# Three plain query groups in place of four, and another order of the closing steps, in a decoder step of two layers

## The chip, the cores and the metric

The kernel runs on one core of a Trainium2 chip. The metric is the device time of one execution in microseconds (us), as the median of several runs; less is better. All arithmetic is in fp32: each matrix operand is split into a high and a low part, and a product is made of three matmuls, high by high, high by low, low by high.

The core's engines run side by side and wait for each other by semaphores: TensorE (PE in the profile, its weight loads PEld), VectorE (DVE), ScalarE (ACT), GpSimd (POOL) and SyncE (SP, which here issues DMAs).

## What is computed

One step of a decoder with mixers of two kinds, over 1024 prompt rows and 8 decoded rows, 2048 wide. Layer 0 (kind A) is a pooling mixer, and layer 1 (kind B) is attention in a window of 128 with its own queries and gates and with keys and values that are projected once. Each ends in a layer norm.

```python
def pool_layer(x, prefix, pos, w_in, w_grp, scale, w_out, g_ln, b_ln):
    z = x @ w_in
    u, gate = z[..., :D_POOL], z[..., D_POOL:]
    d, new_state = multiscale_pool(u, prefix, pos)
    d = jnp.einsum('btgc,gce->btge', d.reshape(B, T, N_POOL_GROUPS, POOL_GROUP), w_grp)
    d = d.reshape(B, T, D_POOL) * scale
    y = (d * jax.nn.silu(gate)) @ w_out
    return layer_norm(ALPHA * x + y, g_ln, b_ln), new_state

def attn_layer(x, pos, kb, vb, k_pos, q_pos, blocked, w_in, sinks, w_out, g_ln, b_ln):
    z = x @ w_in
    q = rope_partial(z[..., :D_ATTN].reshape(B, T, N_HEADS, HEAD_DIM), pos)
    gate = z[..., D_ATTN:]
    ...
    o = attn_core(q, kb, vb, q_pos, k_pos, sinks).reshape(B, T, D_ATTN)
    y = (o * jax.nn.silu(gate)) @ w_out
    return layer_norm(ALPHA * x + y, g_ln, b_ln)
```

The reference calls these once each for the prompt and for the decoded rows, with `shared_kv` (a projection to 4 heads of 64) between them. Outputs are the two results, the new pool states, and the last 128 keys and values.

## The kernel before

The rows are taken in two chunks: chunk 0 has 512 columns in a matmul (rows of the prompt stand along the columns), chunk 1 has 520, the 8 decoded rows among them. The program is one list of stages, `PHASES` (L50): `ai` (input product and pooling), `ao` (output product and layer norm), `bi` (queries, gates and attention), `bo` (output product and layer norm), each with its chunk, and for `ai` and `bi` the range of groups. A group of `bi` is two query tiles and their two gate tiles, of 128 rows each; a tile holds two heads.

A product of a weight with a chunk has two forms. `PLAIN` (L57) names the stages that use the first.

- Plain: `unit` (L672) takes a tile of 128 output rows in 48 matmuls of 512 columns (L686 to L688, the three of one split pair); a group is four units, 192 matmuls.
- Seven products: `seven` (L582) makes, from a block of 2 by 2, seven products in place of eight (the scheme of Strassen). Each product has 24 matmuls (L658 to L660) on half the columns, 256 in chunk 0 and 260 in chunk 1. The seven weights are sums of the four blocks of the weight; they are made by additions (`first_pair`, L346, for chunk 0, which stores them for chunk 1 too) and split into high (L488 on ACT) and low (L503 on DVE). The products are put together by copies on ACT and additions on DVE (`p0` to `p6`, L597 to L631). A group is two such pairs, 336 matmuls. Groups that are plain for chunk 0 have the sums for chunk 1 made in `plain_pair` (L293).

Instructions go to each engine in program order; what sets the order is the code that writes them out. Work beside the products (layer norm of the other chunk, transposes, sums of weights) is in generators. `end` (L527) is called at the end of each product, and four times in a plain unit, and takes one step of the generator at the head whenever `self.i / self.every` passes a whole number, `self.every` being products per step. It is set in `run` (L2148): 3 at the start of each stage, and other values in some.

```python
if self.side and int(self.i / self.every) != int((self.i - 1) / self.every) and room >= self.room:
```

`ln_gen` (L912) is the layer norm of a chunk: its variance's reciprocal root is `rstd` (L901: a lookup on ACT, L904, and three steps on DVE, L905 to L907), then eight pieces of 128x1024 are subtracted and multiplied (L999, L1000 on DVE), scaled (L991 on ACT) and stored. In stage `bo` of chunk 1 it runs for chunk 0, and stores `y0`. There, `shifted` (L1267) sums a pair's columns (`mean` L1276, `less` L1280, `square` L1286, `add` L1291, L1292).

The end of the program is `phase_end` (L1308), for the last three output pairs of chunk 1. Its products follow the table `TAIL`, and `steps` ties closing steps to single products. The columns of chunk 1 are in two halves: A (the last 260, done last) and Bh. For the first, `affine` (L1368: `affine1` subtracts and multiplies on DVE, L1374 and L1375; `affine2` scales and adds on ACT, L1382, and stores, L1383) writes the normed result in the transposed layout. For the last, the results are transposed back: `scale` (L1394, ACT) multiplies by the norm's weights, `turn` (L1477, PE) transposes, `sums_a` (L1432, PE) forms the sums over all rows of the values and of their squares, `moments` (L1437) makes from them the mean and the reciprocal root (L1448 to L1457, L1445), `last_rows` (L1485, PE) subtracts the mean, and `evict` (L1491) multiplies into the output rows, on DVE (L1497) or ACT (L1502), and stores (L1498). `spare` and `last_four` (L1504) do the decoded rows.

## Time and profile before

| | us |
|---|---|
| median of three runs | 2330.92 (2330.76 to 2331.43) |
| the profiled execution | 2332.49 |
| its span, first to last instruction | 2330.7 |

The profile is of one execution. A share is of its span. In a row of the timeline stand the start in us, the duration, the engine, the line, the operation, what it wrote from what (128x260 is partitions by elements) and how often; brackets at its end tell how long the engine stood idle before it and who ended that. `pD`, `pO` and `pS` are accumulators of PE, `m` is a buffer in the on-chip memory. Rows that follow from a view by stretch have the busy time of each engine in that stretch. The granted clock is that of TensorE as a share of full speed. The table below gives the page's costliest lines on DVE and ACT, which stand beside the products.

| line, engine | what | count | busy us |
|---|---|---|---|
| L503, DVE | low part of a weight | 674 | 814.6 |
| L488, ACT | high part of a weight | 674 | 701.5 |
| L778, DVE | low part of an activation | 120 | 147.1 |
| L769, ACT | high part of an activation | 120 | 125.8 |
| L346, DVE | sum of weights | 88 | 107.6 |

### The profile page before, as it was taken

What the parts mean: (1) busy time and instruction counts of PE and PEld (TensorE: products, weight loads), DVE (VectorE), ACT (ScalarE), POOL (GpSimd) and SP (SyncE); (2) the same over time, 40 slices, a digit from 0 to 9 for tenths busy, and PEclk for the clock granted to TensorE, in tenths of its full rate; (3) what the DMA queues carried; (4) which work ended last, traced back from release to release, by engine and by line L of the source; (5) the groups of instructions that cost most, each with busy time, mean ns of one, the idle gap of its engine ahead of it and who ended that gap; (6) DMA issues with size and microseconds to landing.
All of it is one profiled execution on the core that took longest, in us unless ns stands there. A gap on an engine that the chain in (4) does not pass through costs nothing. (4 is left out here: it accounts for less than half of the span.)

```text
span 2330.7 us, 49775 instructions
## 1 busy us (share of the span) xinstructions
PE 2293.2 (98%) x19960; PEld 2199.7 (94%) x19960; DVE 1908.7 (82%) x2422; ACT 1350.4 (58%) x2492; POOL 205.7 (9%) x411
## 2 busy tenths in 40 slices
PE   8999999999999999999999999999999999999997
PEld 6899999999999999999788799999999999999997
DVE  8787998777878878988996888897676777889887
ACT  4444445544546546655465566785776678646556
POOL 0111110010000000000111111100000000000001
PEclk9999999999999999999999999999999999999999
DMA  8668789988899989999886666798777778799785
GB/s 293 221 228 312 267 293 356 330 302 297 278 325 320 340 280 325 323 385 345 274 333 240 241 220 236 240 321 288 246 245 221 221 229 307 243 361 379 250 303 198
DMA packets 250919, 665.04 MB, mean 285 GB/s; under 512 B 25760, under 2 KB 106432, under 8 KB 250688
## 3 DMA queue, kind: packets, MB, share of 16 engines
q1 hardware_dynamic: 205216, 496.79, 63.5%
q0 software_dynamic: 45472, 165.07, 18.4%
q8 instruction: 156, 2.56, 0.4%
q14 instruction: 75, 0.61, 0.1%
HBM read 466.66 MB, written 185.59 MB: 280 GB/s over the span
## 5 line engine op out<-in xcount | busy, mean ns | idle before, releaser
L658 PE MATMUL pD<-m,m 128*128 128x260 f32 (+1 forms) x4752 | 1346.2, 283 | 5.5 <-DVE m L619 3.9
L660 PE MATMUL pD<-m,m 128*128 128x260 f32 (+1 forms) x4752 | 1339.1, 282 | 3.3 <-DVE m L503 3.1
L659 PE MATMUL pD<-m,m 128*128 128x260 f32 (+1 forms) x4752 | 1339.3, 282 | 0.0
L658 PEld LDWEIGHTS pD<-m,m 128*128 128x128 f32 x4752 | 895.3, 188 | 10.9 <-issue 3.2
L660 PEld LDWEIGHTS pD<-m,m 128*128 128x128 f32 x4752 | 895.8, 189 | 4.0 <-DVE m L503 3.9
L659 PEld LDWEIGHTS pD<-m,m 128*128 128x128 f32 x4752 | 895.6, 188 | 0.5
L503 DVE TENSOR_TENSOR m<-m,m 128x1024 fp32r<-128x1024 f32 x674 | 814.6, 1220 | 72.7 <-ACT m L488 48.3
L488 ACT CAST m<-m 128x1024 fp32r<-128x1024 f32 x674 | 701.5, 1048 | 253.1 <-DVE m L346 77.7
L686 PE MATMUL pD<-m,m 128*128 128x512 f32 x448 | 179.7, 401 | 8.0 <-ACT m L769 8.0
L687 PE MATMUL pD<-m,m 128*128 128x512 f32 x448 | 177.6, 396 | 0.7 <-DVE m L778 0.7
L688 PE MATMUL pD<-m,m 128*128 128x512 f32 x448 | 177.2, 396 | 0.0
L778 DVE TENSOR_TENSOR m<-m,m 128x1024 fp32r<-128x1024 f32 (+1 forms) x120 | 147.1, 1229 | 9.5 <-ACT m L769 7.9
L631 ACT COPY m<-pD 128x260 f32<-128x260 f32 (+1 forms) x83 | 31.0, 374 | 189.8 <-PE pD L660 189.7
L769 ACT CAST m<-m 128x1024 fp32r<-128x1024 f32 (+1 forms) x120 | 125.8, 1051 | 10.3 <-DVE m L503 4.1
L346 DVE TENSOR_TENSOR m<-m,m 128x1024 f32<-128x1024 f32 x88 | 107.6, 1223 | 6.9 <-DMA m<-in_wia 4.2
L686 PEld LDWEIGHTS pD<-m,m 128*128 128x128 f32 x448 | 85.0, 190 | 27.9 <-ACT m L769 8.0
L687 PEld LDWEIGHTS pD<-m,m 128*128 128x128 f32 x448 | 85.0, 190 | 20.6 <-DVE m L778 1.9
L688 PEld LDWEIGHTS pD<-m,m 128*128 128x128 f32 x448 | 84.8, 189 | 19.8
L619 DVE TENSOR_TENSOR m<-pD,m 128x260 f32<-128x260 f32 (+1 forms) x86 | 36.5, 425 | 80.9 <-PE pD L660 80.8
L1798 ACT ACTIVATE m<-m,sm 128x128 f32<-128x128 f32 x256 | 99.2, 390 | 0.0
L1820 ACT ACTIVATE m<-m,sm 128x128 f32<-128x128 f32 (+1 forms) x320 | 93.9, 372 | 8.9 <-DVE sm L1806 5.5
L1088 PE MATMUL pD<-m,m 128*128 128x260 f32 (+1 forms) x528 | 91.2, 323 | 0.0
(249 smaller groups left out, 2157.2 us busy)
## 6 DMA issues: line engine op xcount, KB each, us to landing
m<-in_wia SPq DMA_DIRECT2D x124, 512.0 KB
m<-in_wib SPq DMA_DIRECT2D x120, 512.0 KB
swia<-m POOLq DMA_DIRECT2D x64, 512.0 KB, 5.0
m<-swia SPq DMA_DIRECT2D x64, 512.0 KB
m<-swoa SPq DMA_DIRECT2D x64, 512.0 KB
swib<-m POOLq DMA_DIRECT2D x64, 512.0 KB, 5.8
m<-swib SPq DMA_DIRECT2D x64, 512.0 KB
m<-swob SPq DMA_DIRECT2D x56, 512.0 KB
```

Source lines behind the costliest of these rows:

```text
L346: self.nc.vector.tensor_add(s[out].a[:, :1024], s[x].a[:, :1024], s[y].a[:, :1024])
L488: self.nc.scalar.copy(hi.r[:, :1024], self.stream[self.cast].src().a[:, :1024])
L503: self.nc.vector.tensor_sub(lo.r[:, :1024], s.src().a[:, :1024], hi.a[:, :1024])
L658: nc.tensor.matmul(ps[:, :TH], wh[:, s], h, start=new and k == 0, stop=False, skip_group_check=on)
L659: nc.tensor.matmul(ps[:, :TH], wh[:, s], l, start=False, stop=False, skip_group_check=on)
L660: nc.tensor.matmul(ps[:, :TH], wl[:, s], h, start=False, stop=k == 7, skip_group_check=on)
L686: nc.tensor.matmul(ps[:], wh[:, s], h, start=par == 0 and k == 0, stop=False)
L687: nc.tensor.matmul(ps[:], wh[:, s], l, start=False, stop=False)
L688: nc.tensor.matmul(ps[:], wl[:, s], h, start=False, stop=par == 1 and k == 7)
L769: self.nc.scalar.copy(h.r[:, :n], s.a[:, :n])
L778: self.nc.vector.tensor_sub(l.r[:, :n], s.a[:, :n], h.a[:, :n])
L1798: nc.scalar.activation(x["s3"][:, i, :], x["s3"][:, i, :], AF.Exp, bias=nm[:, i : i + 1], scale=0.125, accum_out=rs[:, i : i + 1],)
```

## The change

Three parts. First, the plain `bi` stage of chunk 0 has groups 0 to 2 in place of 0 to 3; group 3 joins the seven-product stage, which has five groups in place of four. Second, `every` has two new values: 1.4 in that seven-product stage (3 before), and 2.4 in `bo` of chunk 1 (3 before). Third, the closing steps of `phase_end` are put in another order: the last product is followed at once by its addition, squares, the transposes and the column sums; two of the subtract-and-multiply steps and their scaling go behind the moments; `scale(y)` goes into the moments; of the eight evictions three, not four, are on DVE.

```diff
@@ -48,8 +48,8 @@
-    ("ai", 0, (0, 1)), ("ai", 0, (1, 4)), ("ai", 1, (0, 4)), ("ao", 0, None), ("ao", 1, None), ("bi", 0, (0, 4)),
-    ("bi", 0, (4, 8)), ("bi", 1, (0, 8)), ("bo", 0, None), ("bo", 1, None),
+    ("ai", 0, (0, 1)), ("ai", 0, (1, 4)), ("ai", 1, (0, 4)), ("ao", 0, None), ("ao", 1, None), ("bi", 0, (0, 3)),
+    ("bi", 0, (3, 8)), ("bi", 1, (0, 8)), ("bo", 0, None), ("bo", 1, None),
@@ -1434,7 +1434,7 @@
-        def moments():
+        def moments(between):
...
             nc.scalar.mul(X[hi], mb[hi, A2], -1.0)
+            between()
@@ -1493,13 +1494,14 @@
+            if k % 2 and (b, k) != (0, 3):
+                nc.vector.tensor_scalar(y, X[b, k][:], r, None, op0=ALU.mult)
+            else:
+                nc.scalar.activation(y, X[b, k][:], AF.Copy, scale=r)
             if k % 2:
-                nc.vector.tensor_scalar(y, X[b, k][:], r, None, op0=ALU.mult)
...
-            else:
-                nc.scalar.activation(y, X[b, k][:], AF.Copy, scale=r)
@@ -1543,15 +1545,13 @@
             (y, 5): [
-                lambda: square(x, A), lambda: affine(0, Bh), lambda: affine(x, Bh), lambda: spare(3), lambda: scale(3),
+                lambda: square(x, A), lambda: affine(0, Bh), lambda: spare(3), lambda: scale(3),
             ],
             (y, 6): [
-                lambda: add(x, A), lambda: rest(z, A), lambda: affine(y, Bh), lambda: spare(x), lambda: scale(x),
+                lambda: rest(z, A), lambda: add(x, A), lambda: affine(x, Bh), lambda: spare(x), lambda: scale(x),
             ],
-            (z, 5): [lambda: square(y, A), lambda: affine(z, Bh), lambda: spare(4), lambda: scale(4)],
-            (z, 6): [
-                lambda: square(z, A, 0), lambda: add(y, A), lambda: scale(z, (0,), True),
-            ],
+            (z, 5): [lambda: square(y, A), lambda: affine1(y, Bh), lambda: spare(4), lambda: scale(4)],
+            (z, 6): [lambda: square(z, A, 0), lambda: add(y, A), lambda: affine2(y, Bh)],
@@ -1567,30 +1567,27 @@
         square(z, A, 1)
-        spare(y)
-        spare(z)
-        scale(z, (1,))
-        scale(y)
-        affine1(1, Bh)
-        affine2(1, Bh)
         X[0, 0], X[0, 1] = self.psD(), self.psD()
         turn(0, 0, 8)
         sums_a(())
         sums_a((0,))
         sums_a((1,))
+        spare(y)
+        spare(z)
+        scale(z, (0, 1), True)
+        affine1(z, Bh)
         X[0, 2], X[0, 3] = self.psW(), self.psW()
+        X[1, 0], X[1, 1] = self.psO(), self.psD()
+        moments(lambda: scale(y))
+        affine2(z, Bh)
         turn(0, 8, 16)
-        X[1, 0], X[1, 1] = self.psO(), self.psD()
         turn(1, 0, 8)
-        affine1(2, Bh)
-        moments()
...
-        affine2(2, Bh)
...
-        affine1(3, Bh)
+        affine1(1, Bh)
@@ -1599,10 +1596,15 @@
         last_rows(1, (3,))
+        affine1(2, Bh)
+        affine2(1, Bh)
+        for k in range(3):
+            evict(1, k)
+        affine2(2, Bh)
+        affine1(3, Bh)
+        evict(1, 3)
         affine2(3, Bh)
         affine1(4, Bh)
-        for k in range(4):
-            evict(1, k)
         affine2(4, Bh)
@@ -2207,6 +2209,8 @@
+            elif (kind, c) == ("bi", 0):
+                self.every = 1.4
@@ -2218,7 +2222,7 @@
-                self.every = 3
+                self.every = 2.4
```

The lines of the new kernel stand one or two later than those of before from L1450 on.

PE, at the place where the third plain group ends after the change (`pD` is a unit's or product's accumulator, `m` are weight and activation). Before, the plain units go on:

```order
L686 MATMUL pD_14584<-m_1487_12538,m_1680_14433 128x512
L687 MATMUL pD_14584<-m_1495_12608,m_1680_14433 128x512
L688 MATMUL pD_14584<-m_1487_12538,m_1684_14481 128x512
L686 MATMUL pD_14584<-m_1496_12610,m_1680_14433 128x512
L687 MATMUL pD_14584<-m_1502_12649,m_1680_14433 128x512
L688 MATMUL pD_14584<-m_1496_12610,m_1684_14481 128x512
```

After:

```order
L686 MATMUL pD_14497<-m_1524_12791,m_1684_14348 128x512
L687 MATMUL pD_14497<-m_1528_12824,m_1684_14348 128x512
L688 MATMUL pD_14497<-m_1524_12791,m_1691_14451 128x512
L658 MATMUL pD_14671<-m_1658_14088,m_1692_14453 128x256
L659 MATMUL pD_14671<-m_1664_14187,m_1692_14453 128x256
L660 MATMUL pD_14671<-m_1658_14088,m_1695_14499 128x256
```

Where a unit of 512 columns stood, the first product of a seven-product pair begins, on 256.

DVE, in stage `bo` of chunk 1, where `ln_gen` takes its reciprocal root (`pD` is a product's accumulator, the 128x1040 rows are the column sums of a pair). Before:

```order
L503 TENSOR_TENSOR m_2848_26616<-m_2829_26465,m_2844_26578 128x1024
L1280 TENSOR_TENSOR m_2795_26196<-m_2795_26196,m_2846_26612 128x1040
L503 TENSOR_TENSOR m_2852_26658<-m_2834_26505,m_2849_26618 128x1024
L1280 TENSOR_TENSOR m_2787_26156<-m_2787_26156,m_2846_26612 128x1040
L503 TENSOR_TENSOR m_2857_26693<-m_2838_26539,m_2853_26660 128x1024
L1291 TENSOR_TENSOR m_2767_26029<-m_2787_26156,m_2795_26196 128x1040
L1292 TENSOR_TENSOR m_2850_26644<-m_2850_26644,m_2854_26687 128x1040
L905 TENSOR_TENSOR m_2845_26606<-m_2793_26192 128x512
L906 SCALAR_TENSOR_TENSOR m_2845_26606<-m_2845_26606 128x512
L907 SCALAR_TENSOR_TENSOR m_2793_26192<-m_2845_26606,m_2793_26192 128x512
L619 TENSOR_TENSOR m_2855_26689<-pD_26572,m_2846_26612 128x260
```

After:

```order
L503 TENSOR_TENSOR m_2860_26789<-m_2842_26644,m_2857_26757 128x1024
L1280 TENSOR_TENSOR m_2805_26365<-m_2805_26365,m_2858_26785 128x1040
L905 TENSOR_TENSOR m_2854_26745<-m_2811_26401 128x512
L906 SCALAR_TENSOR_TENSOR m_2854_26745<-m_2854_26745 128x512
L907 SCALAR_TENSOR_TENSOR m_2811_26401<-m_2854_26745,m_2811_26401 128x512
L503 TENSOR_TENSOR m_2864_26835<-m_2846_26678,m_2861_26791 128x1024
L1280 TENSOR_TENSOR m_2799_26329<-m_2799_26329,m_2858_26785 128x1040
L503 TENSOR_TENSOR m_2869_26870<-m_2850_26712,m_2865_26837 128x1024
L1291 TENSOR_TENSOR m_2779_26202<-m_2799_26329,m_2805_26365 128x1040
L1292 TENSOR_TENSOR m_2862_26817<-m_2862_26817,m_2866_26864 128x1040
L619 TENSOR_TENSOR m_2867_26866<-pD_26751,m_2858_26785 128x260
```

L905 to L907 stand behind the first L1280 now, ahead of two splits, the second L1280, L1291 and L1292; L619 stands behind all of them in both.

ACT, at the same place. Before:

```order
L1276 ACTIVATE m_2846_26612<-pO_26645 128x260
L1276 ACTIVATE m_2846_26612<-pD_26649 128x260
L608 COPY m_2846_26612<-pD_26572 128x260
L488 CAST m_2853_26660<-m_2838_26539 128x1024
L1286 ACTIVATE m_2854_26687<-m_2795_26196 128x1040
L614 COPY m_2855_26689<-pD_26545 128x260
L488 CAST m_2858_26695<-m_2842_26574 128x1024
L1286 ACTIVATE m_2850_26644<-m_2787_26156 128x1040
L904 ACT_TABLE_LOAD
L904 ACTIVATE m_2793_26192<-m_2845_26606 128x512
```

After:

```order
L1276 ACTIVATE m_2858_26785<-pO_26818 128x260
L1276 ACTIVATE m_2858_26785<-pD_26822 128x260
L904 ACT_TABLE_LOAD
L904 ACTIVATE m_2811_26401<-m_2854_26745 128x512
L608 COPY m_2858_26785<-pD_26751 128x260
L488 CAST m_2865_26837<-m_2850_26712 128x1024
L1286 ACTIVATE m_2866_26864<-m_2805_26365 128x1040
L614 COPY m_2867_26866<-pD_26718 128x260
L488 CAST m_2870_26872<-m_2855_26753 128x1024
L1286 ACTIVATE m_2862_26817<-m_2799_26329 128x1040
```

The table load and L904 moved from behind the second L1286 to right behind the second L1276.

DVE, behind the last product, from its addition L612 to the moments (L1449). Before:

```order
L612 TENSOR_TENSOR m_2954_27600<-pD_28018,m_2954_27600 128x260
L1346 TENSOR_TENSOR m_2767_26029<-m_2767_26029,m_2936_27431 128x2x260
L1347 TENSOR_TENSOR m_2850_26644<-m_2850_26644,m_2974_27788 128x2x260
L629 TENSOR_TENSOR m_2954_27600<-pD_28056,m_2954_27600 128x260
L1374 TENSOR_TENSOR m_2975_27790<-m_2975_27790,m_2987_27914 128x2x260
L1375 TENSOR_TENSOR m_2975_27790<-m_2975_27790,m_2987_27914 128x2x260
L1374 TENSOR_TENSOR m_2976_27792<-m_2976_27792,m_2987_27914 128x2x260
L1375 TENSOR_TENSOR m_2976_27792<-m_2976_27792,m_2987_27914 128x2x260
L1449 TENSOR_TENSOR m_2995_28142<-m_2846_26612 128x260
L1451 SCALAR_TENSOR_TENSOR m_2995_28142<-pD_28109,m_2995_28142 128x260
```

After:

```order
L612 TENSOR_TENSOR m_2967_27793<-pD_28189,m_2967_27793 128x260
L1346 TENSOR_TENSOR m_2779_26202<-m_2779_26202,m_2949_27624 128x2x260
L1347 TENSOR_TENSOR m_2862_26817<-m_2862_26817,m_2986_27974 128x2x260
L629 TENSOR_TENSOR m_2967_27793<-pD_28221,m_2967_27793 128x260
L1374 TENSOR_TENSOR m_2967_27793<-m_2967_27793,m_2999_28095 128x2x260
L1375 TENSOR_TENSOR m_2967_27793<-m_2967_27793,m_2999_28095 128x2x260
L1449 TENSOR_TENSOR m_3007_28287<-m_2858_26785 128x260
L1452 SCALAR_TENSOR_TENSOR m_3007_28287<-pD_28265,m_3007_28287 128x260
```

One subtract-and-multiply pair (L1374, L1375) stands between the last addition, L629, and the moments, where there were two.

## The prediction

> **What bounds the kernel now.** I read three views: the page's busy times, the list of what TensorE (PE) waited for, and the busy time of each engine by stretch of the span. In the last, each row gives the stretch, then PE, weight load (PEld), VectorE (DVE), ScalarE (ACT) and GpSimd busy with their counts, then the granted clock, the DMA share and GB/s.
>
> ```profile
> PE 2293.2 (98%) x19960; PEld 2199.7 (94%) x19960; DVE 1908.7 (82%) x2422; ACT 1350.4 (58%) x2492; POOL 205.7 (9%) x411
> PE pD L658 <- DVE m L619: 3.9, 4, 1.3
> PE pO L1863 <- ACT m L1833: 1.8, 1, 1.8
> ```
>
> PE is busy for 98% of the span, and what it waited for comes to single microseconds, so the time is in essence the sum of what PE issues, a few named stalls, and the end behind the last product. DVE, at 82%, is second; where a stretch has it near full, it can take over. So I price the change in three places: the group that changes its form, the last output stage (where side work is taken oftener), and the end.
>
> **1. One plain group becomes a seven-product group.** The plain form takes 192 matmuls of 512 columns for a group; the other takes two pairs of seven products of 24 matmuls, 336, of 256 columns. Their paces are seen in stretches that hold only one kind:
>
> ```profile
> 75.00:100.00 25.00, 25.00 (x110) 20.28 (x109) 17.15 (x16) 10.01 (x11) 2.13 (x4) 1.00 0.53 175
> 875.00:900.00 25.00, 25.00 (x214) 25.00 (x214) 17.01 (x17) 12.85 (x17) 0.53 (x1) 1.00 0.86 296
> 1435.00:1460.00 25.00, 25.00 (x286) 24.72 (x285) 22.59 (x30) 18.45 (x48) 3.63 (x8) 1.00 0.66 228
> ```
>
> A count takes in matmuls still running at an edge; two are left off. Then 25/108 = 231.5 ns for 512 columns and 25/212 = 118 ns for 256. 192 x 0.2315 = 44.4 us go, 336 x 0.118 = 39.6 us come: **-4.8 us** on PE. The attention's own matmuls (L1761, L1863) are the same in number. What hides the rest of the group's work is DVE: the seven-product form adds six weight splits (L488 on ACT, L503 on DVE) and its additions. In the third row, inside the seven-product groups of this stage, PE is busy for all 25.00 us with DVE at 22.59, so there is cover of some 10%, also for the two pieces of the layer norm of chunk 1 that now fall behind the first seven-product group. If that cover goes, the group takes what DVE takes; the nearest row is the first below, where DVE had 24.76 of 25 and PE lost 0.47 us. Bounds: -4.8 and, with two such stretches, -3.8. I take -4.8, by the third row, which is the stage that the new group joins.
>
> Shortly before the plain stage ends there is a stall in the attention between its units, and behind it a slow clock:
>
> ```profile
> 1326.65 0.33 PE L1863 MATMUL pO<-m,m 64*64 64x128 f32 x2 [1.82 <-ACT m L1833]
> 1327.38 0.37 PE L1863 MATMUL pO<-m,m 64*64 64x64 f32 x2 [0.28 <-DVE m L1834]
> ...
> 1325.00:1330.00 5.00, 3.07 (x36) 2.43 (x37) 3.37 (x4) 3.15 (x10) 0.64 (x2) 0.74 1.03 371
> 1330.00:1335.00 5.00, 5.00 (x49) 3.90 (x48) 4.90 (x10) 1.79 (x5) 1.45 (x3) 0.92 1.03 396
> 1335.00:1360.00 25.00, 24.53 (x222) 23.64 (x220) 24.76 (x28) 19.92 (x45) 3.15 (x7) 1.00 0.67 244
> ```
>
> The two waits make 2.10 us; the granted clock is 0.74 and 0.92 in the next two stretches, so (0.26 + 0.08) x 5 = 1.7 us of clock were lost. The same instructions stand there in the same order after the change, one group earlier: I price it at nothing. Its ends are -3.8 (stall and clock loss gone) and +2.1 (the stall doubled); the value taken is the one that the same order gives, and either end needs a cause that the rows don't show.
>
> [...]
>
> **2. The last output stage takes layer-norm steps every 2.4 products, not every 3.** The one step with a new wait is the reciprocal root (L904 on ACT, L905 to L907 on DVE). In the trace of before it stands behind the last additions of a pair:
>
> ```profile
> 2188.95 0.39 ACT L1276 ACTIVATE m<-pD 128x260 f32<-128x260 f32 x1
> 2194.12 1.28 ACT L904 ACT_TABLE_LOAD   x1
> 2195.41 0.63 ACT L904 ACTIVATE m<-m 128x512 f32<-128x512 f32 x1
> ...
> 2189.37 1.24 DVE L1280 TENSOR_TENSOR m<-m,m 128x1040 f32<-128x1040 f32 x1 [1.98 <-ACT m L1276]
> 2196.26 0.68 DVE L905 TENSOR_TENSOR m<-m 128x512 f32<-128x512 f32 x1
> 2198.31 0.42 DVE L619 TENSOR_TENSOR m<-pD,m 128x260 f32<-128x260 f32 x1
> 2198.88 0.36 PE L658 MATMUL pD<-m,m 128*128 128x260 f32 x1 [1.34 <-DVE m L619]
> ```
>
> Now the table load and L904 come on ACT right behind the second L1276, and L905 on DVE behind the first L1280 alone. ACT would end L904 at 2189.34 + 1.28 + 0.63 = 2191.25; DVE ends the first L1280 at 2190.61. So L905 waits some 0.65 us, with the splits and additions of the product queued behind it on DVE, and L619, which releases PE, behind those. The work ahead of L619 is otherwise the same sum in another order. So the stall of 1.34 us grows to about 2.0: **+0.7 us**. Ends: -1.3 in place of +0.7, if the order lets the stall go altogether (DVE stood idle 1.98 us ahead of L1280, and a step that comes sooner could lie there), and +1.7 more, if the clock falls as it did at 2.10 us; both are rivals.
>
> [...]
>
> Then the eight steps that follow (L999, L1000: subtract and multiply a 128x1024 piece) come closer together:
>
> ```profile
> 2205.89 1.22 DVE L999 TENSOR_TENSOR m<-m,m 128x1024 f32<-128x1024 f32 x1
> 2208.29 1.22 DVE L503 TENSOR_TENSOR m<-m,m 128x1024 fp32r<-128x1024 f32 x1
> ...
> 2205.00:2230.00 25.00, 25.00 (x212) 25.00 (x211) 24.68 (x23) 17.05 (x24) 1.07 (x2) 1.00 0.87 310
> 2230.00:2255.00 25.00, 25.00 (x211) 25.00 (x210) 22.83 (x22) 14.27 (x22) 1.58 (x2) 1.00 0.95 342
> ```
>
> A piece takes DVE 2.40 us. A product is 24 matmuls at 25/209 = 0.12 us, 2.87 us, so 25 us hold 8.7 products: 2.9 pieces before, 3.6 after, 0.7 x 2.40 = 1.7 us more DVE work on 24.68 and 22.83, in the mean 25.5 of 25. That is 0.5 us over in 25, while the eight pieces last (8 x 2.4 x 2.87 = 55 us): 1.1 us; products that are ahead in their buffers take up a part. Ends: 0 (by the second row, 24.5 of 25) and 3.0 (by the first, 26.4). I take **+0.3**: the rows' mean holds other extra work (L1280 among it) that does not come in every pair.
>
> **3. The end.** Before, PE transposes behind the last product, waits for DVE, and forms the column sums; the sums lead through ACT and DVE to the moments:
>
> ```profile
> 2306.08 0.60 PE L1477 MATMUL pD<-cst,m 128*128 128x128 f32 x4
> 2307.66 0.66 PE L1477 MATMUL pD<-cst,m 128*128 128x128 f32 x4 [0.98 <-DVE m L612]
> 2308.26 2.46 PE L1432 MATMUL pD<-m,jr 128*128 128x260 f32 x10
> 2311.61 1.58 PE L1432 MATMUL pD<-m,jr 128*128 128x260 f32 x6 [0.89 <-ACT m L1343]
> ...
> 2294.29 1.22 DVE L999 TENSOR_TENSOR m<-m,m 128x1024 f32<-128x1024 f32 x1
> 2308.73 0.42 DVE L629 TENSOR_TENSOR m<-pD,m 128x260 f32<-128x260 f32 x1
> 2314.35 0.35 ACT L1448 COPY m<-pD 128x260 f32<-128x260 f32 x1
> 2318.03 0.87 DVE L1445 TENSOR_TENSOR m<-m,m 32x256 fp32r<-32x256 f32 x2
> ```
>
> The last addition (L629) comes 2.65 us behind the first transpose, since DVE is that far behind: the last of the eight pieces (2294.29) and affine pairs (L1374, L1375) stand ahead of it. The closer pace of part 2 takes the piece from there, and the change puts two of the affine steps behind the moments. So neither the 0.98 nor the 0.89 us should be left: eight transposes from 2306.1 to 2307.0, sixteen sums at (2.46 + 1.58)/16 = 0.25 us to 2311.0, L1448 at 2311.1 (3.25 us sooner). From L1448 to the end of L1445 it was 4.55 us, now to 2315.65. What was moved must then be done:
>
> ```profile
> 2318.93 0.70 DVE L1374 TENSOR_TENSOR m<-m,m 128x520 f32<-128x520 f32 x1
> 2320.28 1.40 DVE L1497 TENSOR_SCALAR m<-pD,sm 128x512 f32<-128x512 f32 x2
> 2321.60 0.21 DVE L1508 TENSOR_TENSOR m<-m 128x64 f32<-128x64 f32 x1
> 2322.52 0.69 DVE L1374 TENSOR_TENSOR m<-m,m 128x520 f32<-128x520 f32 x1
> ...
> 2323.98 1.10 ACT L1382 ACTIVATE m<-m,prm 128x260 f32<-128x260 f32 x2 [0.95 <-DVE m L1375]
> 2324.67 0.99 SPq L1498 DMA_DIRECT2D out_y1a<-m  x2
> 2325.75 0.56 SPq L1383 DMA_DIRECT2D out_y<-m  x1
> 2322.00:2323.00 1.00, 0.00 (x0) 0.00 (x0) 0.93 (x4) 1.00 (x2) 0.00 (x0) 1.00 1.00 401
> 2328.00:2329.00 1.00, 0.00 (x0) 0.00 (x0) 0.00 (x0) 0.00 (x0) 0.00 (x0) 0.50 0.86 307
> ```
>
> An affine pair is 1.35 us (from 2318.93 to 2320.28), an eviction 0.66, the four small steps 0.92. Behind the moments DVE now has four pairs, three evictions and the small steps: 5.4 + 2.0 + 0.9 = 8.3 us, to 2323.95; the last two L1382 on ACT 1.10, to 2325.05; the last store is issued some 0.65 us sooner than at 2325.75. Then the queue: before, two stores of 0.5 MB went out at 2324.67 just ahead of it, and transfers ran until about 2328.9 at 400 and 307 GB/s. Now an affine pair and its scaling lie between the last large store and the last one, so up to 0.5 MB/0.4 = 1.3 us of queue goes; I take 0.9. Sum **-1.6**. Ends: -0.6 (issue alone) and -2.0.
>
> **Sum.** -4.8 + 0.7 + 0.3 - 1.6 = -5.4. The profiled execution took 2332.49 us (span 2330.7 and 1.79 around it), 1.57 above the median of 2330.92: 2332.49 - 5.4 = 2327.1, and less the same 1.57, **2325.5**. The 1.57 is about one slow-clock stretch, which may not be in every execution.
>
> **The rivals.**
> - The clock falls at the longer L619 stall, too. For it: it comes to 2.0 us, and 2.10 sufficed. Against it:
>
> ```profile
> 2190.00:2215.00 25.00, 23.66 (x197) 23.48 (x196) 23.78 (x24) 16.68 (x22) 1.07 (x2) 1.00 0.80 262
> ```
>
> with 1.34 us of stall inside, the clock stayed at 1.00. It gives +1.7: 2327.2. Chance 0.21.
> - The swap or the end brings less, DVE being the bound in the new group (-3.8) or behind the moments (-0.6, or evictions on ACT late): +1.0 to +2.0, some 2327.8 with a part of part 2's upper end. Chance 0.15.
> - ACT pauses behind the table load before L904 begins, for about another 1.28 us as the load itself takes; L905, the additions and L619 are later by as much: +1.3, 2326.8. The row of L904 shows no such pause. Chance 0.02. [...]
> - The L619 stall vanishes and the end takes its full -2.0: -0.7 - 1.3 - 0.4 = -2.4, 2323.1. Chance 0.12.
> - Slower: in the last output stage DVE at 26.4 of 25 becomes the bound, and what it is late is not spread but gathers in stalls of 2 us at every second of the eight pieces. Each then costs 2.1 and a slow stretch of 1.7: 4 x 3.8 = 15.2, 2340. It decides from a lateness of some 2 us at one product; the excess by the first row is 3.0 us over all eight, 0.4 each, which speaks against it. Chance 0.04.
> - The change does nothing: the group is no shorter since PE then waits for weights (the DMA share is 0.66 in the stage). 2331. Chance 0.02.
>
> **How the numbers follow.** The forecast's own case has 0.44. What a measurement of this kernel can tell from no change is about 0.2%, 4.7 us: faster means below 2326.3. Of the first case 0.39 lies below that and 0.05 above, by its terms' ends; with the 0.12 that is 0.51 faster; 0.05 + 0.21 + 0.15 + 0.02 + 0.02 = 0.45 the same; 0.04 slower. The range goes from 2322.8, just beyond the third rival, to 2329.2: the second rival with the upper end (3.0) of the piece term half taken. It leaves out the slower case, no effect, and some 0.1 on the edges.
>
> **What would show it.** In the changed kernel's profile: 64 fewer each of L686 to L688, and PE busy for 25.00 of 25 in the seven-product groups of the first attention stage; the stall of about 2 us at L1863 with the slower clock behind it, about a group's time earlier; L905 waiting for L904 and L619 releasing PE after about 2 us, with the clock at 1.00 there; the last L999 before 2270; sums right behind the transposes, L1448 some 3 us closer to the last product, and the last landing 1.6 us closer. The forecast is wrong if PE shows waits for DVE in stretches where it now has none, or if the clock falls a second time in the last stage.

## The result and the profile after

The changed kernel took 2338.27 us (median of 8; 2334.41 to 2341.26) against 2332.32 for the kernel before (median of 8; 2330.76 to 2334.48): ratio 1.0025, 95% interval 1.0016 to 1.0034. A second comparison gave 2336.07 against 2332.52, ratio 1.0020 (1.0011 to 1.0029). It is slower by 3.5 to 6 us, where 5.4 less was forecast. Of the rivals, the first (the clock falls at the longer L619 stall) happened in the profile, but it gave 2327; most of the loss is elsewhere.

The profiled execution took 2339.09 us, its span 2337.3, 6.6 more than that of before. First what TensorE waited for, as groups of line and releaser (total, count, longest), in the changed kernel:

```profile
PE pD L658 <- DVE m L619: 6.1, 5, 2.5
PE pD L660 <- DVE m L503: 4.7, 2, 2.7
PE pO L1865 <- ACT m L1835: 4.1, 2, 2.9
```

The same three groups were 3.9, 3.1 (two waits, the longest 2.6) and 1.8 us before; the third is L1863 there. The page's busy share of PE is 98% in both kernels, and cannot show this: it counts a matmul at half clock as busy (4.46 of the 5.00 us from 1235 us, at a clock of 0.50). So the second view is the stalls one by one, with the granted clock (third number from the end) of the 5 us behind each, in the changed kernel:

```profile
1232.89 0.33 PE L1865 MATMUL pO<-m,m 64*64 64x128 f32 x2 [2.90 <-ACT m L1835]
1235.54 1.88 PE L1763 MATMUL pS<-m,m 64*64 64x192 f32 x20 [0.80 <-DVE m L1731]
1279.49 0.33 PE L1865 MATMUL pO<-m,m 64*64 64x128 f32 x2 [1.25 <-ACT m L1835]
2035.54 0.46 PE L658 MATMUL pD<-m,m 128*128 128x256 f32 x1 [2.45 <-DVE m L619]
2108.23 0.39 PE L660 MATMUL pD<-m,m 128*128 128x256 f32 x1 [2.69 <-DVE m L503]
2205.23 0.36 PE L658 MATMUL pD<-m,m 128*128 128x260 f32 x1 [2.07 <-DVE m L619]
...
1230.00:1235.00 5.00, 1.58 (x32) 1.15 (x32) 2.10 (x4) 4.12 (x8) 0.10 (x1) 0.85 0.16 62
1235.00:1240.00 5.00, 4.46 (x65) 3.75 (x66) 3.61 (x5) 2.63 (x4) 0.00 (x0) 0.50 0.32 105
1280.00:1285.00 5.00, 4.79 (x35) 3.85 (x36) 4.97 (x6) 0.99 (x6) 0.65 (x2) 0.66 1.04 363
2035.00:2040.00 5.00, 4.46 (x25) 4.49 (x26) 4.97 (x7) 0.99 (x1) 1.06 (x2) 0.66 1.01 375
2105.00:2110.00 5.00, 2.31 (x20) 2.10 (x19) 4.96 (x7) 1.27 (x2) 0.58 (x2) 1.00 1.04 392
2205.00:2210.00 5.00, 4.77 (x27) 4.80 (x28) 4.97 (x6) 0.92 (x2) 0.00 (x0) 0.66 0.81 296
```

Four of the six are followed by a slow clock: (0.15 + 0.50) x 5 = 3.2 us behind the first pair, 0.34 x 5 = 1.7 behind each of three others. Two rows of before, at the places where the fourth and fifth stand now, for comparison; both had the clock at 1.00 behind them:

```profile
2034.25 0.36 PE L658 MATMUL pD<-m,m 128*128 128x256 f32 x1 [1.33 <-DVE m L619]
2103.34 0.39 PE L660 MATMUL pD<-m,m 128*128 128x256 f32 x1 [0.56 <-DVE m L503]
```

The end came out nearly as long as forecast (what made it so is another matter, see the parts alone). From the timeline of the changed kernel:

```profile
2313.98 1.04 PE L1478 MATMUL pD<-cst,m 128*128 128x128 f32 x8
2314.85 3.67 PE L1432 MATMUL pD<-m,jr 128*128 128x260 f32 x16
2318.12 0.38 ACT L1448 COPY m<-pD 128x260 f32<-128x260 f32 x1 [2.18 <-PE pD L1432]
2321.82 0.87 DVE L1445 TENSOR_TENSOR m<-m,m 32x256 fp32r<-32x256 f32 x2
2330.24 2.38 SPq L1383 DMA_DIRECT2D out_y<-m  x2
2334.00:2335.00 1.00, 0.00 (x0) 0.00 (x0) 0.00 (x0) 0.00 (x0) 0.00 (x0) 0.50 0.37 98
```

Transposes and sums run through. From the first transpose to the end of the span it is 2337.3 - 2313.98 = 23.3 us, before 2330.7 - 2306.08 = 24.6: -1.3. All that precedes the transposes is therefore 7.9 us later (2313.98 - 2306.08). In that: the swap's matmuls, -4.8; stalls of the first attention stage, 2.90 + 0.80 + 1.25 and two of 0.28 for 2.10, +3.4; the clock there, 4.9 for 1.7, +3.2; the two stalls in the first chunk's output stage +3.3 and the clock +1.7; L619 in the last stage +0.7 and the clock +1.7. That is 9.2; early in the program a slow stretch of before (1.7 us, behind a stall at 355 us, which neither kernel's change touches) is missing in this profile, which leaves 7.5 of 7.9. That is one execution: in a second profile of the same kernel (span 2333.9) the transposes begin 4.7 us later than in the first profile of before.

### The profile page after: what moved, and what is told of

Same layout as the page of the kernel before. It is cut to its first block, busy times and chain, and to the rows that moved or that the text cites. A ratio compares the mean times of both kernels' runs of the same rounds, so it can differ in the third digit from the quotient of the medians.

```text
span 2337.3 us, 50083 instructions
## 1 busy us (share of the span) xinstructions
PE 2293.3 (98%) x20104; PEld 2208.7 (94%) x20104; DVE 1915.0 (82%) x2427; ACT 1358.0 (58%) x2504; POOL 204.3 (9%) x411
## 3 DMA queue, kind: packets, MB, share of 16 engines
q0 software_dynamic: 45472, 165.07, 18.3%
## 5 line engine op out<-in xcount | busy, mean ns | idle before, releaser
L658 PE MATMUL pD<-m,m 128*128 128x260 f32 (+1 forms) x4864 | 1379.2, 284 | 8.7 <-DVE m L619 6.1
L660 PE MATMUL pD<-m,m 128*128 128x260 f32 (+1 forms) x4864 | 1371.4, 282 | 4.9 <-DVE m L503 4.7
L659 PE MATMUL pD<-m,m 128*128 128x260 f32 (+1 forms) x4864 | 1371.5, 282 | 0.0
L658 PEld LDWEIGHTS pD<-m,m 128*128 128x128 f32 x4864 | 917.0, 189 | 14.4 <-issue 6.3
L660 PEld LDWEIGHTS pD<-m,m 128*128 128x128 f32 x4864 | 917.8, 189 | 5.6 <-DVE m L503 5.5
L659 PEld LDWEIGHTS pD<-m,m 128*128 128x128 f32 x4864 | 917.4, 189 | 0.5
L503 DVE TENSOR_TENSOR m<-m,m 128x1024 fp32r<-128x1024 f32 x680 | 820.8, 1218 | 70.2 <-ACT m L488 46.6
L686 PE MATMUL pD<-m,m 128*128 128x512 f32 x384 | 154.7, 403 | 8.0 <-ACT m L769 8.0
L687 PE MATMUL pD<-m,m 128*128 128x512 f32 x384 | 152.9, 398 | 0.5 <-DVE m L778 0.5
L688 PE MATMUL pD<-m,m 128*128 128x512 f32 x384 | 152.7, 398 | 0.0
L769 ACT CAST m<-m 128x1024 fp32r<-128x1024 f32 (+1 forms) x120 | 125.8, 1052 | 10.9 <-DMA m<-in_x 4.0
L346 DVE TENSOR_TENSOR m<-m,m 128x1024 f32<-128x1024 f32 x96 | 117.3, 1222 | 10.2 <-DMA m<-in_wia 6.1
L619 DVE TENSOR_TENSOR m<-pD,m 128x260 f32<-128x260 f32 (+1 forms) x88 | 37.2, 423 | 84.3 <-PE pD L660 84.2
L686 PEld LDWEIGHTS pD<-m,m 128*128 128x128 f32 x384 | 73.3, 191 | 25.3 <-ACT m L769 8.0
L1088 PE MATMUL pD<-m,m 128*128 128x260 f32 (+1 forms) x528 | 91.2, 323 | 0.0
L687 PEld LDWEIGHTS pD<-m,m 128*128 128x128 f32 x384 | 73.4, 191 | 17.4 <-DVE m L778 1.0
L688 PEld LDWEIGHTS pD<-m,m 128*128 128x128 f32 x384 | 73.2, 191 | 17.1
```

The lines of the kernel that those rows point to most:

```text
L346: self.nc.vector.tensor_add(s[out].a[:, :1024], s[x].a[:, :1024], s[y].a[:, :1024])
L503: self.nc.vector.tensor_sub(lo.r[:, :1024], s.src().a[:, :1024], hi.a[:, :1024])
L658: nc.tensor.matmul(ps[:, :TH], wh[:, s], h, start=new and k == 0, stop=False, skip_group_check=on)
L659: nc.tensor.matmul(ps[:, :TH], wh[:, s], l, start=False, stop=False, skip_group_check=on)
L660: nc.tensor.matmul(ps[:, :TH], wl[:, s], h, start=False, stop=k == 7, skip_group_check=on)
L686: nc.tensor.matmul(ps[:], wh[:, s], h, start=par == 0 and k == 0, stop=False)
```

## The experiments

Theory A in them is that the swap pays what was forecast, and that two losses take it away: a weight that comes late at the end of the plain stage, and the pace of 2.4 in the last stage, each dearer by a slow clock behind its stall. A ratio is to the kernel before in the same comparison, with its 95% interval; 11 or 12 executions of each version, 33 to 35 of the kernel before. An interval reaches some 2 us to each side, so a difference of some 2 us between two versions lies at the edge of the noise.

| kernel | median us | before | ratio |
|---|---|---|---|
| swap and 1.4 alone | 2334.68 | 2333.44 | 1.0002 (0.9994 to 1.0010) |
| pace 2.4 alone | 2331.62 | 2333.44 | 0.9992 (0.9983 to 1.0000) |
| closing order alone | 2331.62 | 2333.44 | 0.9990 (0.9981 to 0.9998) |
| the same, again | 2332.09 | 2332.65 | 0.9996 (0.9987 to 1.0004) |
| whole change, again | 2336.07 | 2332.52 | 1.0020 (1.0011 to 1.0029) |
| whole, pace 3 | 2333.70 | 2332.52 | 1.0006 (0.9997 to 1.0015) |
| whole, no swap | 2334.27 | 2332.52 | 1.0006 (0.9997 to 1.0014) |
| whole, loads later | 2333.06 | 2332.52 | 1.0002 (0.9993 to 1.0011) |
| whole, loads later, start one sooner | 2332.29 | 2332.65 | 1.0000 (0.9991 to 1.0008) |
| whole, loads later, pace 3 | 2329.50 | 2332.65 | 0.9986 (0.9977 to 0.9994) |
| swap, loads later | 2328.89 | 2332.65 | 0.9987 (0.9978 to 0.9995) |

### The parts alone

The swap, as a diff against before:

```diff
-("bi", 0, (0, 4)), ("bi", 0, (4, 8))
+("bi", 0, (0, 3)), ("bi", 0, (3, 8))
...
+            elif (kind, c) == ("bi", 0):
+                self.every = 1.4
```

> Of the change, only the third-to-fourth plain group's swap (PHASES) and the value 1.4 in the seven-product stage. Theory A: the swap itself pays its 4.8 us of matmuls, but the end of the plain stage now has a stall of about 3 us of TensorE (a weight that lands late) and two slow stretches of the clock in place of one; in sum +1 us against before (-2 to +3). Rival B: the swap pays its 4.8 us, and the loss of the whole change sits in the last output stage: -4.8 us.

The swap alone is +1.2 us in the median, and its interval takes in no change: A's number, not B's. Its profile has the same stall, with two steps of slow clock behind it. From the waits of TensorE (two waits, the longest 2.5 us):

```profile
PE pO L1863 <- ACT m L1833: 3.8, 2, 2.5
```

The pace alone:

```diff
-                self.every = 3
+                self.every = 2.4
```

> Of the change, only the pace 2.4 in place of 3 in the last output stage. Theory A: the stall at L619 grows from 1.3 to 2 us, with a slow stretch of 1.7 behind it in some executions: +0.5 to +2.5 us. Rival B: the layer-norm pieces make DVE the bound there, +8 us or more. A second rival: the stall goes, -1.3.

The result is 0.9992 (0.9983 to 1.0000), a small gain if any. A and B missed; the second rival's -1.3 lies in the interval, but its mechanism failed: the stall did not go. The profile has 2.27 us at L619 in place of 1.34, with a slow stretch behind it. What it gains is at the end of the program (below).

The closing order alone is the third part of the change's diff.

> Of the change, only the order of the closing steps. Theory A and B alike: from the last product's end to the last instruction 23.3 in place of 24.6 us, as in the profile of the whole change: -1.3 us. Rival: without the closer pace DVE is still behind at the last product, and the transposes and sums wait as before: -0.3 us.

> The closing order alone, for the second time. Theory A: 1.3 to 1.8 us under before. Rival: the first result was chance; within 0.5 us of before.

0.9990 and 0.9996: between -2.3 and -0.9 us, so -1.3 fits, and the rival of -0.3 is not excluded. The profiles say more. From the first transpose behind the last product I took the time to SyncE's last store and to the end of the span (us; one profile each, two where two numbers stand):

| kernel | to the last store | to the end |
|---|---|---|
| before | 19.7, 19.7 | 24.6, 24.9 |
| closing order alone | 19.2, 19.2 | 24.0, 24.2 |
| swap, old order | 18.0 | 23.2 |
| swap, loads later, old order | 17.9 | 23.3 |
| pace 2.4, old order | 16.4 | 21.9 |
| pace 2.4, new order (no swap) | 18.3 | 24.0 |
| whole change | 18.3, 18.3 | 23.3, 23.2 |
| whole, loads later, pace 3 | 18.3 | 23.6 |

The two rows of the pace alone, old order:

```profile
2308.94 1.03 PE L1477 MATMUL pD<-cst,m 128*128 128x128 f32 x8
2325.30 0.58 SPq L1383 DMA_DIRECT2D out_y<-m  x1
```

With the closing steps in their old order the pace alone shortens the end by 2.7 us, and the swap alone by 1.4: the last layer-norm piece (L1000) starts 56 us ahead of the first transpose with the pace, 17 with the swap, 11 before, so it is out of DVE's way at the end. To the last store, the new order gains 0.4 us on the kernel before; it loses 0.3 with the swap, and 1.9 with the pace. So the shorter end of the whole change does not need the new order.

The kernel before, once more:

> The kernel before, unchanged, for a second profile. Theory A: stalls stand where they stood, with the same lengths within 0.3 us where the order of instructions alone sets them, and the clock falls behind some that it did not fall behind the first time, and the other way: 2331 to 2335 us. Rival: the same stalls always have the same clock behind them.

Its median was 2333.22. The stalls that the order sets were there again (1.34 us at L619 in the last stage, 1.82 in the attention); the one in the first chunk's output stage was 1.96 us this time, not 1.33:

```profile
2031.91 0.36 PE L658 MATMUL pD<-m,m 128*128 128x256 f32 x1 [1.96 <-DVE m L619]
```

So that stall differs by 0.6 us from one execution to the next without any change. It was 1.2 to 2.4 us in the six profiles without the swap and 2.1 to 2.5 in the eight with it, so a share of the swap is not excluded. The other of the two, 2.69 us at 2108 us, follows a step on DVE that waited for a load:

```profile
2104.34 0.43 DVE L826 TENSOR_TENSOR m<-m 128x260 f32<-128x260 f32 x1 [4.36 <-DMA m<-o]
```

In the second profile of the changed kernel that wait was 1.78 us, and no stall of 0.5 us or more followed. Side steps on DVE stand elsewhere in this stage with the swap, so the change may have a part in it. How much of the first profile's +3.3 us is the change's stays open.

### The whole change, less one part

```diff
-                self.every = 2.4
+                self.every = 3
```

> The whole change without the pace 2.4 (it is 3 again). The swap shortens a stage by two products' places, so that side steps fall on other products in every later stage; with 3 the reciprocal root then stands behind L619 and not ahead of it. Theory A (pace and swap cost time only together): no stall at L619 near 2200 us, about 2333 us, 5 less than the whole change. Rival: the loss sits in the swap's stage alone; 2338 as the whole change.

> The whole change again, beside its parts. Theory A: 2336 to 2340 us as measured, with the stall of over 2 us at L1865 near 1230 us and the one at L619 near 2203 us again, each with a slow clock behind it in most executions. Rival: the first eight runs lay high by chance; then 2331, the sum of the parts (swap +1.2, pace -1.8, end -1.8 on 2333.4).

2333.70 against 2336.07: the pace costs 2.4 us here by medians, half of what A expected; the two intervals overlap a little. The whole change is slower again, so its first result was no chance. Its second profile has 1.77 us at L1865 near 1230 us (2.90 the first time) and 1.25 at L1763, with a slow clock behind, and 2.05 us at L619 without one. The waits of PE within the last output stage (2130 to 2300 us), in this second profile and with pace 3:

```profile
PE pD L658 <- DVE m L619: 3.1, 2, 2.1
PE pD L660 <- DVE m L503: 1.2, 2, 0.8
```

```profile
PE pD L658 <- ACT m L769: 1.0, 1, 1.0
PE pD L660 <- DVE m L503: 0.8, 1, 0.8
PE pD L658 <- DVE m L619: 0.2, 1, 0.2
```

With the swap and pace 3, L905 to L907 fall behind L619 and L624, since the swap leaves two product places fewer (14 for 16 in a group) ahead of every later side step; there the stall of 1.34 us that the kernel before has goes too.

Without the swap (the first two hunks of its diff undone):

> The whole change without the swap and the value 1.4: pace 2.4 and the closing order alone. Theory A (parts add where the swap is not): 2333.4 - 1.8 - 1.8 = 2329.8 us. Rival: the two gains are the same one (DVE is less behind at the last product), and together they give no more than one: 2331.6.

2334.27, where 2329.8 or 2331.6 was expected. Both numbers missed. Its profile has 2.27 us at L619 and a slow stretch behind it, and no other new wait in that stage. Pace and closing order do not add. A part of that stands in the table of the end: with the pace, the new order issues the last store 1.9 us later than the old one, and the end is 2.1 us longer. By the medians, each against before, both together are 3.6 us slower than the pace alone (+1.8 and -1.8); the rest of that is within the noise.

### The late weight

The chain behind the first stall, in the profile of the whole change, is read on two engines: ScalarE's row that waited longest there, and what SyncE issued before it.

```profile
1230.88 1.04 ACT L488 CAST m<-m 128x1024 fp32r<-128x1024 f32 x1 [6.06 <-DMA m<-in_wib]
...
1198.33 3.07 SPq L287 DMA_DIRECT2D m<-in_wib  x2
1201.51 0.86 SPq L759 DMA_DIRECT2D m<-h  x1
1209.31 0.37 SPq L759 DMA_DIRECT2D m<-th  x1
1209.87 0.43 SPq L759 DMA_DIRECT2D m<-h  x1
1210.71 0.34 SPq L287 DMA_DIRECT2D m<-in_wib  x1
1212.21 1.29 SPq L759 DMA_DIRECT2D m<-th  x1
1213.60 5.36 SPq L1616 DMA_DIRECT2D m<-m  x4
```

ACT has its cast of a weight at the head of its queue and waits 6.06 us for the load; the copy L1835 that TensorE needs is queued behind that cast. SyncE issues no DMA from 1202.37 to 1209.31, ahead of a load of `th`, an activation of the next stage (L759), and weight loads (L287) stand behind that. What that load waited for, by the waits of SyncE:

```profile
SPq L759 <- DMA swib<-m: 6.8, 1, 6.8
```

`swib` is a store of a sum of weights; so it was, as far as the profile infers it, a buffer that a store still held, and not the data of `th`. The same releaser ended a wait of 4.7 to 6.6 us there in three other profiles with the swap and the early loads. The weight that the cast waited for was issued at 1219.88, by the trace, and landed at 1230.80, 10.9 us later: the DMA engines' busy share is 1.00 to 1.05 from 1195 to 1225 us. In the kernel before, the next stage's loads began one group later, at 1239.71. There, too, the first of them was held, for 8.5 us; but the DMA share was 0.36 to 0.82 from 1240 to 1260 us, and no stall followed. So I moved their start:

```diff
-                if t == 2 * ps[-1] - 1:
+                if t == 2 * ps[-1]:
                     self.x_begin(nxt)
```

> The whole change, with the next stage's activation loads (x_begin, L759) begun one tile, two units, later in the last plain group. Theory A (the loads block SyncE's queue ahead of the weight load that ACT waits for near 1230 us): the stall of 2.9 us at L1865 and its two slow windows (3 us) go, 4 to 6 us less than the whole change. Rival: the weight is late because the DMA engines are full there (0.96 to 1.06), whatever the order; the stall stays within 0.5 us, or comes back at the first products of the next stage.

3.0 us less than the whole change in the same comparison, where A expected 4 to 6. SyncE's rows in its profile:

```profile
1201.48 11.16 SPq L287 DMA_DIRECT2D m<-in_wib  x5
1212.76 1.06 SPq L992 DMA_DIRECT2D h<-m  x1
1214.21 4.27 SPq L1616 DMA_DIRECT2D m<-m  x4
1218.58 1.12 SPq L287 DMA_DIRECT2D m<-in_wib  x1
1225.43 0.38 SPq L759 DMA_DIRECT2D m<-th  x1
```

Five weight loads go out ahead of the activation, within 11 us, and the stall near 1230 us is gone, as A said, though the DMA share is 0.98 to 1.03 from 1195 to 1225 us here too. So full DMA engines alone do not make that stall; the order on the queue does, with them. The rival is right in part: at the next stage's beginning a stall stands that was not there, and takes back some of it:

```profile
1304.32 0.55 PE L658 MATMUL pD<-m,m 128*128 128x256 f32 x1 [2.79 <-ACT m L1800]
```

### Both losses taken away

> The whole change with the later activation loads (as in e8) and with pace 3 in place of 2.4 (as in e5). Theory A (two separate losses, each with its slow clock): the two gains add, 2336.1 - 3.0 - 2.4 = 2330.7 us, and no stall over 1 us near 1230 or 2200 us. Rival (one loss takes the other's place): 2333, no better than either alone.

2329.50, ratio 0.9986 (0.9977 to 0.9994): faster than before, and 6.6 us under the whole change by medians (pace -2.4, loads -3.0, sum -5.4 expected). The two losses add, as far as the noise lets it be told. The stall at the next stage's beginning (2.51 us) stays.

> The swap with 1.4 and the later activation loads, nothing else of the change. Theory A: the swap's 4.8 us of matmuls come through but for what is left of the stalls in the hand-over (e8's profile has 2.8 us at L658 and a slow window of 1.5 there, in place of 2.1 and 1.7 of before): 2 to 4 us under before. Rival: no gain is left, within 0.5 us of before.

2328.89, ratio 0.9987 (0.9978 to 0.9995), 3.8 us under before. With its own late weight out of the way, most of the swap's 4.8 us arrives; the swap alone was 1.2 us over before, so by medians the later loads are worth 5.0 us to it (two comparisons). These two are the versions whose gain over the kernel before is clear of noise, by 0.1%; between them no difference can be told. The closing order's gain alone was clear in one comparison and not in the other.

### The pace or the place

```diff
-                self.at(3, lambda gen=gen: add("y", gen))
+                self.at(2, lambda gen=gen: add("y", gen))
```

> As e8, and the layer-norm generator of the last output stage starts one product earlier, with pace 2.4: the reciprocal root then stands behind the first of a pair's L1237 and far ahead of L619. Theory A (its place decides, not the pace): the stall at L619 near 2197 us is under 0.5 us, and the time 2 us below e8, 2331. Rival (the closer pace makes DVE late whatever the place): a stall of 1 us or more for DVE in the stage all the same, 2333.

2332.29, and the stall at L619 was 1.72 us with L905 to L907 far ahead of it: the rival. The stage from 2190 us, by 25 us, first this kernel (pace 2.4), then the one with pace 3 and the loads later:

```profile
2190.00:2215.00 25.00, 22.19 (x182) 21.70 (x180) 24.78 (x23) 16.16 (x21) 0.54 (x1) 1.00 0.94 307
2215.00:2240.00 25.00, 24.97 (x208) 24.97 (x209) 24.71 (x24) 17.53 (x24) 0.91 (x2) 1.00 1.00 365
```

```profile
2190.00:2215.00 25.00, 24.74 (x207) 24.56 (x207) 24.64 (x26) 15.02 (x19) 0.54 (x1) 1.00 0.78 257
2215.00:2240.00 25.00, 25.00 (x211) 25.00 (x210) 22.26 (x23) 15.35 (x23) 1.58 (x2) 1.00 0.99 367
```

DVE (third busy number) is full for 50 us with the closer pace, and PE loses 2.8 us; with 3 it has 2.7 us to spare in the second half, and PE loses 0.3. In the first half, where the stall lies, DVE's load is the same (24.78 and 24.64), so the load is not all. In this profile a piece of the layer norm (L999, L1000, 2.40 us) stands between the two L1280 ahead of L619, where the root stood in the whole change; with pace 3 two shorter steps (L955, L978, 1.40 us) stand ahead of L619. So it is not the root's place alone. These rows fit that the length of side work ahead of L619 decides, over 2 us in both versions with pace 2.4; whether the pace could be kept with less there was not run.

## Why the prediction was wrong

1. **The swap, -4.8: right in size.** 336 matmuls on 256 columns for 192 on 512; in the first profile the new group has no wait for DVE above 0.44 us. In the second it has one of 1.70 us at L619 (1307.90), so the cover by DVE is not always there. The swap with the loads later brings 3.8 of it.
2. **"I price it at nothing" was the step that failed.** The prediction took the end of the plain stage as the same instructions in the same order, one group earlier. They are so on PE, and on ACT and DVE but for some side steps; on SyncE the next stage's activation loads came a group earlier too, into a stretch in which the DMA engines are full (busy share 1.00 to 1.05; 0.36 to 0.82 where those loads stood before), with weight loads behind them in the one queue. That made a stall of 2.90 us out of none, beside the old one (1.25 + 0.28 here): with all waits there +3.4 us of stalls and, in the first profile, +3.2 us of clock, in place of nothing. The prediction counted what moved on the engines and not what was moved ahead of a weight on the queue. Taking the loads back is worth 3.0 us in the whole change and 5.0 to the swap alone.
3. **The last stage, +0.7 + 0.3.** L905 waited 0.70 us for L904, where 0.65 was worked out, and the stall was 2.07 us, where 2.0 was: the mechanism was right, step for step:

```profile
2194.91 1.28 ACT L904 ACT_TABLE_LOAD   x1
2196.21 0.63 ACT L904 ACTIVATE m<-m 128x512 f32<-128x512 f32 x1
2196.87 0.69 DVE L905 TENSOR_TENSOR m<-m 128x512 f32<-128x512 f32 x1 [0.70 <-ACT m L904]
2204.67 0.42 DVE L619 TENSOR_TENSOR m<-pD,m 128x260 f32<-128x260 f32 x1
```

 The load's end (2196.19) and L904's start (2196.21) are 0.02 us apart: the pause of some 1.28 us that one rival had there did not come. But the comparison was with the wrong alternative. The swap moves every later side step, so that with pace 3 the step would have fallen behind L619 with no stall; the pace costs 2.4 us by that measure, not 1.0. Behind that stall the eight pieces cost little: in the four profiles with pace 2.4 and the swap PE waits once at most, for L503, by 0.8 to 1.1 us in three of them and not at all in the first; the +0.3 that was taken is nearer than the upper end (3.0). And the pace had a gain that the sum did not price apart from the closing order: the shorter end.
4. **The clock, priced as a rival with 0.21.** It is not one case among others: four slow stretches stand in the first profile of the changed kernel before its end, two in that of before, and this is worth 4.9 us of the 7.9. In the second profile of the changed kernel there are two, in that of before one, so the 4.9 is one execution's share and no fixed cost. The prediction took the length of a stall as the condition; in the profiles the idle time within one step of 3.413 us told the cases apart better (below).
5. **The end, -1.6: near in number, partly by luck.** It is -1.3 in the profile. The moments were ready 8.7 us behind the first transpose (2322.69 - 2313.98; forecast 9.6, before 12.8), and PE's two waits went, as forecast. But the last store was issued 1.4 us sooner, not 0.65, and of the 0.9 us of queue nothing came: from there to the end it is 5.1 us, before 4.9 (the share of the DMA engines is still 1.06 in the last full microsecond, 2333 to 2334). And the shorter end is not the new order's: the swap alone has it with the old one (23.2 us), and with the pace the old order's end is shorter still (21.9).
6. The range, 2322.8 to 2329.2, had no room for a new stall outside the three places that were priced.

## What to carry to other kernels

When a stage is shortened, follow the DMA issues as closely as the engines: a prefetch that begins "one group before the end" moves with the end, and whatever stands behind it in a queue moves back (here SyncE issued nothing for 6.9 us, and TensorE stood 2.90 us for it). A counter that paces side work shifts in all later stages, too, so a new pace must be compared with where the steps would now fall, not with where they stood. Parts that all relieve one engine at the end of a program (here DVE) should be priced together, since the first of them can take the gain of the others (to the end of the span the pace alone took 2.7 us off, and with the new order the end was 2.1 us longer again). And a stall of some 2 us on TensorE should be priced with the slow clock that can follow it (1.7 us for a stretch, in these profiles).

## What the runs showed of the hardware

In thirteen of fourteen profiles (the other has one slow stretch alone, at the end) all slow stretches of the clock begin whole multiples of 3.413 us apart, within 0.001 of a step. In the whole change they begin at 1233.51, 1281.29, 2035.64, 2206.31 and 2329.19 us, in the first profile of before at 358.01, 1327.39 and 2324.08. The clock is 0.50 in each of these. Before the end each lasts one step or two: 6.83 us at 1233.51, 3.41 at the others. Where these steps lie against the program's start differs from one profile to the next: counted back from the slow stretches, the first step begins at 1.29 us in the whole change and at 3.02 in before.

I divided all fourteen from 100 to 2300 us by these steps and summed TensorE's idle time in each. In 26 steps it was 1.98 us or more, and a slow step followed every one. In 36 it was 1.20 to 1.85 us, and a slow step followed four, all four at the small attention matmuls (64 x 64). Below 1.2 none began one in a clock at full speed. In the first profiles of before and of the whole change the five steps with 2.07, 2.10, 2.45, 2.56 and 2.96 us of idle time were followed by a slow one; those with 1.32 and 1.78, with 128x128 matmuls alone, were not, and the one with 1.52, at the small matmuls, was. None of the 26 steps from 1.20 to 1.85 us without small matmuls began a slow one, so between 1.85 and 1.98 us these counts change from none to all there; more than the counts is not shown. With small matmuls it was four of ten, and what decides there stays open: one step of 1.48 us idle was followed by a slow one (loads later, pace 3), and one of the same idle time and the same small matmuls was not (loads later, start one sooner). The stall of 1.82 us at the attention was followed by a clock of 0.66 in the repeat of the kernel before, and of 1.00 with the closing order alone; its step has small matmuls behind the stall in the first and none in the second.

So in these profiles the steps into which the idle time of a stall falls tell the cases apart. Both cases stand in the first list of the changed kernel's stalls: the 2.45 us at 2035.54 lie within one step, and a slow one follows; the 2.69 us at 2108.23 fall into two, 1.78 and 0.91, and the clock stays at 1.00.

The times of one kernel can differ by this from one execution to the next (2329.6 to 2338.6 for the kernel before in one comparison), as a slow step of 3.413 us at a clock of 0.50 costs 1.7 us, and a stall near 2 us had one behind it or not: the two profiles of before have two slow steps and one, and spans of 2330.7 and 2329.2. That this makes the whole spread is not shown.

Open are why two steps of equal idle time at the small matmuls are followed by different clocks, how far the swap makes the two stalls in the first chunk's output stage longer, and what the swap, the pace and the later loads would give with the closing steps in their old order, which no run has.
